# A two-layer diffusion backbone: q of the next HGRN2 head projected ahead of its gates, and a 32-byte tile at the right end of SBUF

## The chip, the cores and the metric

The kernel runs on one core of a Trainium2 chip. Its time is the device time of one execution in microseconds (us), and the figure for the kernel before is the median of three runs. The profile is of one further execution, whose own time stands beside it below.

A core has five engines with an instruction queue each: TensorE (PE in the profile; PEld is its weight load), VectorE (DVE), ScalarE (ACT), GpSimd (POOL) and SyncE (SP, which here issues DMAs). SBUF is the on-chip memory of 128 partitions, and an address below is a byte offset in each partition. PSUM is the memory into which TensorE accumulates.

## The reference

Two layers work on 1024 latent tokens and 256 context tokens of width 1024. Layer 0 runs neighbourhood attention heads and mLSTM heads side by side. Layer 1, which the change touches, has 16 HGRN2 heads with key and value widths of 128, and only its latent tokens are an output:

```python
q, f_fwd, f_bwd, i, z = split(h @ w_in)              # 5 x 2048 columns; 128 of each per head
f = lb + (1 - lb) * sigmoid(f_pre)                   # per direction
k, lf = 1 - f, log(f)
q = silu(q)
# each direction d: the state over the context tokens, then chunk by chunk over the latent tokens
o = q exp(b) @ S + (causal pairs q exp(b_t - b_s) k) @ v;   S = exp(b_L) S + (k exp(b_L - b))^T v
out = rms(o_fwd + o_bwd) * h_norm * silu(z)
x = x + gate * (concat(out) @ w_out)
```

Here b is the running sum of lf. The kernel works with products of f instead of sums of its logarithm.

## The kernel before

**Projections.** Matmuls of large operands are done in three products: an operand is split into a high part and a low part, and `dense` (L125 to L131) issues high x high (L128), high x low (L129) and low x high (L130) for each of 8 blocks of 128 rows. The modulated input of a layer stands in `hh` and `hl` (8 x 1280 columns). `proj_tr` (L143) keeps a 128-column slab of the weight stationary and moves `hh`/`hl`, 256 or 512 tokens at a time; the profile names these matmuls mm<-hh,wh (the moving operand comes first). `proj_nat` (L134) keeps tokens stationary and moves the weight (mm<-wh,hh, mm<-wzh,hh).

**Weights.** `wring` loads a weight of 128 columns in two pieces of four row blocks. A piece is a DMA on SP's queue into a raw buffer (three of them), a cast on ACT into a tile `wh` (L72) and a subtraction on DVE into `wl` (L73). In layer 1 these tiles are a ring of four of each on the right side of SBUF (pool w1); in layer 0 the ring is on the left side (pool w0). The v and z columns of a head have tiles of their own on the left side (`wz`).

**SBUF.** Pools are laid from the left or from the right end. `hh` and `hl` are on the right side, and so are the ring of layer 1 and the pool `oy` of the output projections (tiles wo, y, oacc). Before, hh starts at 147424 in one layer and 131040 in the other; the ring's first tiles of layer 1 are at 221152 and 227296. All of these are 32 more than a multiple of 64. The tiles on the left start at multiples of 64.

**A head.** The loop (L1339 to L1352) does for each head:

- `hg_intra`: K = 1 - F from the gates F of both directions (L972), Q = q x F (L979), 16 small "strips" s<-gq,gkn (L997) for the pairs nearest to each other, and then seven levels (`hg_level`), each with an ACT copy of K (gksel, L1024), 16 strips s<-gQ,gksel, a copy under a mask (L1042), and the updates of K and Q by the products of f (L1050, and T at L1052).
- `hg_vz`: the projection of v and z: 24 matmuls mm<-hh,wz for the context's v (its transposes tr<-ident,gEc come later), then 8 tiles of tokens with 24 mm<-wz,hh each. `hg_close` transposes K (L1009).
- `hg_ctx`: the state over the context. Its k lies in a buffer of the tag gq, which has two buffers, shared with the two halves of q. The transposes are L954, the copy gknc L956, the matmuls s<-gv,gknc L961.
- `hg_scan`: the states chunk by chunk (L1062 and L1078 on PE, L1064 and L1080 on DVE) and the outputs (acc, L1073 to L1075). For each half of the chunks four squares on ACT (L1089) give sums gss, POOL takes them to the power -1/2 (L154, L156), and DVE multiplies the output by it and by z (gz, L1093).
- `hg_proj` for the next head: six projections of gates (per direction 256 context tokens and twice 512 latent tokens, 24 matmuls each, a sigmoid L899 and a scaling L900), then q (twice 512 latent tokens, a sigmoid L908 and a multiply L909).
- `hg_out`: transposes of gz (L1133), an ACT copy gyt (L1135) and a store.
- `wo_sums` (L1101 to L1116): work for the end of the kernel on POOL's queue, loads of quarters of the output weight into the buffers gknc and gEc, subtractions and stores; one per head for heads 0 to 7, two for heads 8 to 11. `y_diff` (heads 1 to 8) is similar.

Afterwards `hh` and `hl` are freed, and the output projection (L835 to L837) runs with loads into `oy`.

**Order.** A tile scheduler orders the instructions of every engine: it goes by the order of the program text as priority and by a timeline of its own of when operands and buffers come free. So the matmuls of a head's projections stand between the strips and transposes of the head before it. PSUM has two banks for projections (mm), two for transposes (tr), three for s and one for acc. The gates have one buffer each (gF, gFc), and so have gK, gQ, gEc and gknc.

Of the kernel before, what the change touches and what calls it, by code (L numbers as in the profile page):

```python
# [9 lines left out]
F32 = mybir.dt.float32  # L10
F32R = mybir.dt.float32r
U8 = mybir.dt.uint8
AF = mybir.ActivationFunctionType
ALU = mybir.AluOpType
# [4 lines left out]
P = 128  # L19
D = 1024  # L20
KD = D // P
LAT = 1024
CTX = 256
# [21 lines left out]
class Prog:  # L45
# [836 lines left out]
    def hg_proj(self, h, pool, w=None):  # L882
        nc, a = self.nc, self.a
        st = {}
        col = lambda i: a["wc"][:, i * 2048 + h * P : i * 2048 + (h + 1) * P]
        lb, olb = self.lb[:, 0, h : h + 1], self.lb[:, 1, h : h + 1]
        F = self.t(self.fp, [P, 2, LAT], F32, "gF", 1)
        Fc = self.t(self.fp, [P, 2, CTX], F32, "gFc", 1)
        todo = [(d, t0, n) for d in range(2) for t0, n in ((LAT, CTX), (512, 512), (0, 512))]
        if w:  # L890

            todo.sort(key=lambda x: x[1] == 0)
        w = w or [None, None]
        for d, t0, n in todo:
            w[d] = w[d] or self.wring([col(1 + d)], P)
            ps = self.ps("mm", [P, n])
            self.proj_tr(ps, w[d], 0, t0, n)
            dst = Fc[:, d, :] if t0 == LAT else F[:, d, t0 : t0 + 512]
            nc.scalar.activation(dst, ps, AF.Sigmoid)  # L899
            nc.vector.tensor_scalar(out=dst, in0=dst, scalar1=olb, scalar2=lb, op0=ALU.mult, op1=ALU.add)  # L900
        q = {}
        w = self.wring([col(0)], P)
        for t0 in (512, 0):
            ps = self.ps("mm", [P, 512])
            self.proj_tr(ps, w, 0, t0, 512)
            q[t0 // 512] = self.t(pool, [P, 512], F32, "gq", 2)
            sg = self.t(pool, [P, 512], F32, "gsg", 1)
            nc.scalar.activation(sg, ps, AF.Sigmoid)  # L908
            nc.vector.tensor_tensor(out=q[t0 // 512], in0=sg, in1=ps, op=ALU.mult)  # L909
        return dict(F=F, Fc=Fc, q=q)  # L910

    def hg_vz(self, h, st, pool):
# [55 lines left out]
    def hg_intra(self, st, pool):  # L968
        nc = self.nc
        F, q = st["F"], st["q"]  # L970
        K = self.t(pool, [P, 2, LAT], F32, "gK", 1)
        nc.vector.tensor_scalar(out=K, in0=F, scalar1=-1.0, scalar2=1.0, op0=ALU.mult, op1=ALU.add)  # L972
        Q = self.t(pool, [P, 2, LAT], F32, "gQ", 1)
        ks = [self.t(pool, [P, 512], F32, "gkn", 4) for _ in range(2)]
        for hf in (1, 0):
            s = slice(hf * 512, (hf + 1) * 512)
            nc.vector.tensor_tensor(out=ks[hf], in0=K[:, 0, s], in1=K[:, 1, s], op=ALU.add)
            for d in range(2):
                nc.vector.tensor_tensor(out=Q[:, 1 - d, s], in0=q[hf], in1=F[:, d, s], op=ALU.mult)  # L979
        hv = dict(Q=Q, K=K, T=F, D=self.t(pool, [P, 8, 64], F32, "gD", 1))  # L980
        hv["A"] = self.t(pool, [P, 8, P], F32, "gA", 1)
# [157 lines left out]
    def build(self):  # L1139
        tc, nc, a = self.tc, self.nc, self.a  # L1140
        dma = nc.sync.dma_start
        with ExitStack() as es:
# [22 lines left out]
            def load(name, shape, eng=nc.gpsimd):  # L1165
# [12 lines left out]
                out=self.qkn, in0=qkn[:, 0:1], scalar1=qkn[:, 1:2], scalar2=0.125, op0=ALU.mult, op1=ALU.mult  # L1178
# [3 lines left out]
            sg = self.t(cp, [P, KD, 2], F32, "sct")  # L1182
# [10 lines left out]
            for i in range(2):  # L1193
# [6 lines left out]
                out=self.lb[:, 1, :], in0=self.lb[:, 0, :], scalar1=-1.0, scalar2=1.0, op0=ALU.mult, op1=ALU.add  # L1200
            )


            right = ExitStack()
            es.enter_context(right)
            self.open_h(right)
# [76 lines left out]
            with tc.tile_pool(name="op0", bufs=2) as op, ExitStack() as wl:  # L1283
# [27 lines left out]
                right = es.enter_context(ExitStack())  # L1311
# [22 lines left out]
            with l1:  # L1334
                pool = l1.enter_context(tc.tile_pool(name="hg", bufs=2))
# [32 lines left out]
                w = block(W[0:D, 0:512], wo * 8, None, [self.rawp, 3, "wraw"])  # L1368
                self.out_part(w, 0, 0, y2, yp, lambda t, ps: nc.scalar.copy(acc[0][:, t, :], ps))
                w = block(self.sw[1], wr * 4 + wo * 4)  # L1370
# [233 lines left out]
```

## Time and profile before

| | us |
|---|---|
| median of three runs | 3487.19 (3485.26 to 3489.89) |
| the profiled execution, its own time | 3489.74 |
| its span in the profile | 3488.0 |
| busy: PE / DVE / ACT / POOL | 3409.5 / 2098.0 / 1478.0 / 707.3 |
| first strips of head 0 | at 1898.3 |
| first strips of head 15 | at 3248.1 |

The mean granted clock of TensorE in that execution was 0.993 of full speed. A row of a timeline reads: start, duration, engine, line, operation, out<-in, tile shape and count, and in brackets the idle time before it with what ended it. A row of a group reads: line, engine, operation, operands, shape, count, then busy time, mean ns, and the idle time before them. An instruction's duration of a matmul reaches over its successor's start, so that the time which a matmul costs is read from the distance between starts.

### The profile page before, as it was taken

How to read it: one execution, taken by the hardware profiler on the slowest of the kernel's cores; microseconds unless marked ns; L12 is line 12 of the kernel's file. 1: busy time of each engine (PE TensorE's matmuls, PEld its weight loads, DVE VectorE, ACT ScalarE, POOL GpSimd, SP SyncE). 2: the span in 40 equal slices, each digit the busy share in tenths (PEclk: the TensorE clock that was granted, in tenths of full speed). 3: DMA queues.
4: the chain of work that ended last, by engine and by line, in shares of the span. 5: the costliest groups of instructions: out<-in, count | busy, mean ns of one | idle time of the engine just before them, and what ended most of it. 6: DMA issues, size and time to landing. Idle time of an engine off the chain costs nothing.

```text
span 3488.0 us, 64893 instructions
## 1 busy us (share of the span) xinstructions
PE 3409.5 (98%) x25100; PEld 2990.6 (86%) x25100; DVE 2098.0 (60%) x4855; ACT 1478.0 (42%) x3433; POOL 707.3 (20%) x1076
## 2 busy tenths in 40 slices
PE   8999999999999999999999999999999999999997
PEld 5679998889989888898888988988888888888876
DVE  4546665666655566777666555555555555555667
ACT  5445554554543444454354333333333333333442
POOL 2222221222111112221100112222223222100023
PEclk9999999999999999999999999999999999999999
DMA  5542222322233434444752111111112111110274
GB/s 202 175 130 61 79 77 76 91 78 75 79 89 99 145 117 127 132 129 143 218 162 70 46 58 55 58 59 58 57 57 67 61 58 49 49 37 31 85 233 151
DMA packets 331540, 333.60 MB, mean 96 GB/s; under 512 B 30984, under 2 KB 277960, under 8 KB 331232
## 3 DMA queue, kind: packets, MB, share of 16 engines
q1 hardware_dynamic: 291008, 222.76, 22.0%
q0 software_dynamic: 40224, 106.69, 9.0%
q8 instruction: 198, 3.24, 0.4%
q14 instruction: 110, 0.90, 0.1%
HBM read 259.40 MB, written 69.79 MB: 94 GB/s over the span
## 4 chain that ended last, share of the span: by engine, by line
PE 85%; DMA 4%; issue 3%; DVE 3%; POOL 2%; ACT 1%; SPq 0%; POOLq 0%; DVEq 0%; ACTq 0%
PE mm L128 18%; PE mm L129 18%; PE mm L130 18%; PE s L997 4%; PE acc L775 2%; PE mm L837 2%; PE mm L835 2%; PE mm L836 2%; PE tr L755 2%; PE acc L547 2%; PE s L556 2%; PE acc L537 1%; PE tr L1009 1%; PE acc L1073 1%; PE acc L1074 1%
## 5 line engine op out<-in xcount | busy, mean ns | idle before, releaser
L128 PE MATMUL mm<-hh,wh 128*128 128x512 f32 (+1 forms) x1600 | 584.5, 365 | 0.0
L129 PE MATMUL mm<-hl,wh 128*128 128x512 f32 (+1 forms) x1600 | 584.3, 365 | 0.0
L130 PE MATMUL mm<-hh,wl 128*128 128x512 f32 (+1 forms) x1600 | 583.5, 365 | 0.0
L128 PE MATMUL mm<-wh,hh 128*128 128x256 f32 (+1 forms) x1520 | 471.2, 310 | 1.7 <-ACT ev L317 0.6
L129 PE MATMUL mm<-wl,hh 128*128 128x256 f32 (+1 forms) x1520 | 469.9, 309 | 0.0
L130 PE MATMUL mm<-wh,hl 128*128 128x256 f32 (+1 forms) x1520 | 468.9, 309 | 0.3 <-DVE hl L262 0.3
L130 PEld LDWEIGHTS mm<-hh,wl 128*128 128x128 f32 x1600 | 301.3, 188 | 45.6 <-issue 0.6
L129 PEld LDWEIGHTS mm<-hl,wh 128*128 128x128 f32 x1600 | 301.6, 188 | 43.8 <-issue 0.2
L128 PEld LDWEIGHTS mm<-hh,wh 128*128 128x128 f32 x1600 | 301.6, 188 | 43.0 <-issue 0.2
L128 PEld LDWEIGHTS mm<-wh,hh 128*128 128x128 f32 x1520 | 286.5, 189 | 16.5 <-issue 0.9
L129 PEld LDWEIGHTS mm<-wl,hh 128*128 128x128 f32 x1520 | 286.5, 188 | 14.7 <-issue 2.9
L130 PEld LDWEIGHTS mm<-wh,hl 128*128 128x128 f32 x1520 | 286.4, 188 | 13.8 <-issue 1.5
L128 PE MATMUL mm<-wzh,hh 128*128 128x256 f32 x1024 | 292.8, 286 | 0.6 <-ACT gz L934 0.6
L129 PE MATMUL mm<-wzl,hh 128*128 128x256 f32 x1024 | 292.8, 286 | 0.0
L130 PE MATMUL mm<-wzh,hl 128*128 128x256 f32 x1024 | 291.5, 285 | 0.0
L73 DVE TENSOR_TENSOR wl<-wraw,wh 128x512 fp32r<-128x512 f32 x240 | 165.5, 694 | 129.2 <-ACT wh L72 121.5
L72 ACT CAST wh<-wraw 128x512 fp32r<-128x512 f32 x240 | 147.2, 618 | 198.9 <-PE mm L129 140.7
L1024 ACT COPY gksel<-gK 128x1024 f32<-128x1024 f32 x112 | 128.0, 1143 | 213.0 <-PE s L997 139.2
L128 PEld LDWEIGHTS mm<-wzh,hh 128*128 128x128 f32 x1024 | 193.5, 189 | 3.8 <-ACT gz L934 1.6
L129 PEld LDWEIGHTS mm<-wzl,hh 128*128 128x128 f32 x1024 | 193.4, 189 | 1.0
L130 PEld LDWEIGHTS mm<-wzh,hl 128*128 128x128 f32 x1024 | 193.3, 189 | 1.0
L835 PE MATMUL mm<-woh,yh 128*128 128x512 f32 x422 | 170.4, 404 | 9.8 <-DVE og L1366 5.2
(390 smaller groups left out, 7623.4 us busy)
## 6 DMA issues: line engine op xcount, KB each, us to landing
wraw<-in_wab_dram SPq DMA_DIRECT2D x112, 256.0 KB
wraw<-in_wc_dram SPq DMA_DIRECT2D x96, 256.0 KB
wraw<-yd SPq DMA_DIRECT2D x94, 256.0 KB
adar<-in_wada_dram POOLq DMA_DIRECT2D x32, 512.0 KB, 4.5
wraw<-in_wc_dram SPq DMA_DIRECT2D x128, 128.0 KB
md<-ev POOLq DMA_DIRECT2D x60, 256.0 KB, 2.8
mloz<-md SPq DMA_DIRECT2D x40, 256.0 KB
adar<-in_wada_dram SPq DMA_DIRECT2D x16, 512.0 KB
```

The costliest lines, as they stand in the source:

```text
L72: nc.scalar.copy(hi, x)
L73: nc.vector.tensor_tensor(out=lo, in0=x, in1=hi.bitcast(F32), op=ALU.subtract)
L128: mm(ps, lhsT=lh(k), rhs=rh(k), start=(start and k == 0), stop=False)
L129: mm(ps, lhsT=lh(k), rhs=rl(k), start=False, stop=False)
L130: m = mm(ps, lhsT=ll(k), rhs=rh(k), start=False, stop=(stop and k == nk - 1))
L547: nc.tensor.matmul(num, lhsT=qc[:, j, :], rhs=C[d][:, j, :], start=False, stop=(j == 1))
L556: nc.tensor.matmul(u, lhsT=st["k"][c][:, j * P : (j + 1) * P], rhs=vw, start=True, stop=True)
L755: nc.tensor.transpose(pt[:nk, i, :], pr[:, o : o + nk], self.ident)
L775: m = nc.tensor.matmul(yp[h64], lhsT=v[:, h64], rhs=pTs[hd][:nk, i, :], start=(i == turn[0]), stop=(i == turn[-1]), tile_position=(0, hd * ...
L835: mm(ps, lhsT=yh[k], rhs=w.h(kk), start=(kk == 0), stop=False)
L997: self.nc.tensor.matmul(out[s], lhsT=lhsT, rhs=rhs, start=True, stop=True, tile_position=(0, b * 64))
L1024: nc.scalar.copy(ksel.rearrange("p (b s i) -> p b s i", s=2, i=h), pick(K))
```

## The change

It has two parts.

In `hg_proj` the q projection becomes an inner function `swish()`. Its instructions are the same: a weight slab of 128 columns with its two loads, casts and subtractions, 48 matmuls of 512 columns, two sigmoids and two multiplies. For heads 1 to 15 (no weight handed in) it is called ahead of the six gate projections; for head 0, whose gate weights are loaded earlier and handed in, it stays behind them.

In `build` a pool `edge` is opened on the right side ahead of `hh` and `hl`, with one tile of 8 fp32 columns (32 bytes in each partition), which DVE sets to zero once. All that lies on the right side moves down by 32 bytes: hh to 147392 and 131008, the ring's first tiles in layer 1 to 221120 and 227264. The tiles on the left stay where they were.

The number of instructions on each engine is the same but for that one on DVE.

```diff
--- before.py
+++ after.py
@@ -884,12 +884,27 @@
         st = {}
         col = lambda i: a["wc"][:, i * 2048 + h * P : i * 2048 + (h + 1) * P]
         lb, olb = self.lb[:, 0, h : h + 1], self.lb[:, 1, h : h + 1]
+        q = {}
+
+        def swish():
+            w = self.wring([col(0)], P)
+            for t0 in (512, 0):
+                ps = self.ps("mm", [P, 512])
+                self.proj_tr(ps, w, 0, t0, 512)
+                q[t0 // 512] = self.t(pool, [P, 512], F32, "gq", 2)
+                sg = self.t(pool, [P, 512], F32, "gsg", 1)
+                nc.scalar.activation(sg, ps, AF.Sigmoid)
+                nc.vector.tensor_tensor(out=q[t0 // 512], in0=sg, in1=ps, op=ALU.mult)
+
+        todo = [(d, t0, n) for d in range(2) for t0, n in ((LAT, CTX), (512, 512), (0, 512))]
+        if w:
+
+            todo.sort(key=lambda x: x[1] == 0)
+        else:
+            swish()
         F = self.t(self.fp, [P, 2, LAT], F32, "gF", 1)
         Fc = self.t(self.fp, [P, 2, CTX], F32, "gFc", 1)
-        todo = [(d, t0, n) for d in range(2) for t0, n in ((LAT, CTX), (512, 512), (0, 512))]
-        if w:
-
-            todo.sort(key=lambda x: x[1] == 0)
+        first = w
         w = w or [None, None]
         for d, t0, n in todo:
             w[d] = w[d] or self.wring([col(1 + d)], P)
@@ -898,15 +913,8 @@
             dst = Fc[:, d, :] if t0 == LAT else F[:, d, t0 : t0 + 512]
             nc.scalar.activation(dst, ps, AF.Sigmoid)
             nc.vector.tensor_scalar(out=dst, in0=dst, scalar1=olb, scalar2=lb, op0=ALU.mult, op1=ALU.add)
-        q = {}
-        w = self.wring([col(0)], P)
-        for t0 in (512, 0):
-            ps = self.ps("mm", [P, 512])
-            self.proj_tr(ps, w, 0, t0, 512)
-            q[t0 // 512] = self.t(pool, [P, 512], F32, "gq", 2)
-            sg = self.t(pool, [P, 512], F32, "gsg", 1)
-            nc.scalar.activation(sg, ps, AF.Sigmoid)
-            nc.vector.tensor_tensor(out=q[t0 // 512], in0=sg, in1=ps, op=ALU.mult)
+        if first:
+            swish()
         return dict(F=F, Fc=Fc, q=q)
 
     def hg_vz(self, h, st, pool):
@@ -1201,6 +1209,8 @@
             )
 
 
+            edge = es.enter_context(tc.tile_pool(name="edge", bufs=1, side="right"))
+            nc.vector.memset(self.t(edge, [P, 8], F32, "edge"), 0.0)
             right = ExitStack()
             es.enter_context(right)
             self.open_h(right)
```

More of the change, by code (lines that the diff above doesn't have):

```diff
@@ L886, in hg_proj @@
         lb, olb = self.lb[:, 0, h : h + 1], self.lb[:, 1, h : h + 1]
-        F = self.t(self.fp, [P, 2, LAT], F32, "gF", 1)
-        Fc = self.t(self.fp, [P, 2, CTX], F32, "gFc", 1)
+        q = {}
[8 more added lines that the diff above has]
+                nc.vector.tensor_tensor(out=q[t0 // 512], in0=sg, in1=ps, op=ALU.mult)
         todo = [(d, t0, n) for d in range(2) for t0, n in ((LAT, CTX), (512, 512), (0, 512))]
@@ L892, in hg_proj @@
             todo.sort(key=lambda x: x[1] == 0)
+        else:
+            swish()
+        F = self.t(self.fp, [P, 2, LAT], F32, "gF", 1)
+        Fc = self.t(self.fp, [P, 2, CTX], F32, "gFc", 1)
+        first = w
         w = w or [None, None]
```

## The prediction

> **What bounds the kernel now.** I read the page first: the busy shares, then the chain of waits.
>
> ```profile
> PE 3409.5 (98%) x25100; PEld 2990.6 (86%) x25100; DVE 2098.0 (60%) x4855; ACT 1478.0 (42%) x3433; POOL 707.3 (20%) x1076
> PE 85%; DMA 4%; issue 3%; DVE 3%; POOL 2%; ACT 1%; SPq 0%; POOLq 0%; DVEq 0%; ACTq 0%
> ```
>
> TensorE is busy for 98% of the span and holds 85% of the chain that ended last. Both programs issue the same matmuls, so the change can act in three ways: on the time from one matmul to the next, on the few places where PE waits, and on the clock. Next comes the view by stretches, cut where a head's first strips start (columns: length; busy time of PE, PEld, DVE, ACT, POOL; clock; DMA share; GB/s).
>
> ```profile
> 1898.30:2698.80 800.50, 789.64 (x7016) 717.38 (x7016) 450.88 (x734) 281.61 (x583) 172.76 (x235) 1.00 0.18 57
> 2254.10:2343.10 89.00, 87.44 (x781) 79.44 (x780) 50.54 (x83) 31.70 (x66) 19.94 (x27) 1.00 0.18 57
> 2698.80:3160.10 461.30, 451.06 (x3893) 404.91 (x3892) 254.34 (x415) 158.20 (x331) 85.29 (x126) 0.99 0.16 50
> 3160.10:3248.10 88.00, 86.45 (x773) 78.46 (x772) 47.45 (x79) 29.44 (x62) 8.37 (x11) 1.00 0.08 25
> 3248.10:3488.00 239.90, 212.76 (x1229) 173.26 (x1228) 167.76 (x241) 92.98 (x180) 63.07 (x59) 0.95 0.55 170
> 2794.10:2797.40 3.30, 3.30 (x18) 3.30 (x17) 0.87 (x3) 0.86 (x2) 0.00 (x0) 0.50 0.00 0
> ```
>
> Row one is heads 0 to 8, row two one of them (head 4), row three heads 9 to 13, row four head 14, row five head 15 and the last projection. A steady head takes 89.0 us, but heads 9 to 13 take 461.3 / 5 = 92.3. The last row is a piece of head 10 in which the granted clock was 0.50.
>
> In a steady head PE waits once. The timelines of PE, ACT, POOL and DVE:
>
> ```profile
> 2261.52 0.39 PE L1075 MATMUL acc<-gS,gQ 128*128 128x128 f32 x2
> 2266.47 0.49 PE L1133 MATMUL tr<-ident,gz 128*128 128x128 f32 x3
> 2268.40 1.18 PE L997 MATMUL s<-gQ,gksel 128*64 128x64 f32 x32 [1.45 <-DVE gQ L1050]
> ```
> ```profile
> 2262.01 0.28 ACT L1089 ACTIVATE gjk<-acc 128x128 f32<-128x128 f32 x1 [1.79 <-PE acc L1075]
> ```
> ```profile
> 2263.98 1.36 POOL L156 TENSOR_TENSOR gss<-gss,mhalf 128x4 f32<-128x4 f32 x1
> ```
> ```profile
> 2265.38 1.13 DVE L1093 SCALAR_TENSOR_TENSOR gz<-acc,gss,gz 128x128 f32<-128x128 f32 x4 [0.59 <-POOL gss L156]
> 2267.03 1.22 DVE L1050 TENSOR_TENSOR gQ<-gQ,gF 128x1024 f32<-128x1024 f32 x1
> ```
>
> The previous head's last accumulation (2261.52) starts a chain: squares on ACT, the power on POOL, four gz multiplies on DVE, and behind these gQ's update for level 1. Only six transposes stand on PE between the strips of level 0 and those of level 1, so PE waits 1.45 us.
>
> Heads 9 to 13 have a second wait, from POOL's queue (PE, then POOL):
>
> ```profile
> 2792.73 0.81 PE L1133 MATMUL tr<-ident,gz 128*128 128x128 f32 x3 [1.87 <-DVE gz L1093]
> ```
> ```profile
> 2771.00 1.13 POOL L1109 DMA_DIRECT2D gknc<-in_woc_dram  x2 [40.52 <-ACT gsg L908]
> 2789.61 0.19 POOL L154 TENSOR_SCALAR gss<-gss 128x4 f32<-128x4 f32 x1 [1.85 <-ACT gjk L1089]
> 2789.88 0.73 POOL L1110 TENSOR_TENSOR gEc<-gEc 128x256 f32<-128x256 f32 x1
> 2791.17 1.03 POOL L156 TENSOR_TENSOR gss<-gss,mhalf 128x4 f32<-128x4 f32 x1
> 2792.17 0.59 POOL L1116 DMA_DIRECT2D sw<-gEc  x1
> ```
>
> From head 8 to 11 two wo_sums are issued per head. Here they hold POOL from 2771.0 to 2792.8, 21.8 us, and a subtraction and a store stand between the two halves of gss. PE waits 1.87 us, and the 0.50 clock follows at 2794.1: 3.4 us at half speed lose 1.7.
>
> **The change, part by part.** *Order.* I compared the two built programs: TensorE's instructions are the same up to head 1's first gate, and SP's for its first 918 of 1014. In a steady head, runs of matmuls of one kind go from 58 to 65. I priced every pair of neighbours by its mean start-to-start time over heads 2 to 8 of the trace, some 780 matmuls each; no single row shows these prices, but their sum can be held against one: before's order costs 87.49 us a head by them, with the wait of 1.45 it is 88.94, and row two has 89.0. After's order costs 88.90: seven more switches at 0.2 us each, 1.41. In after, 35 wz matmuls stand between the two levels, 35 x 0.117 = 4.1 us (spacing below) in place of six transposes, and that covers the 1.45. So **a steady head gains next to nothing**: the wait is turned into switches. Heads 0 to 8 come to 801.3 against 800.5: +0.8.
>
> For heads 9 to 13, after's order is priced at 447.7 against 461.3, **-13.6**, if POOL's wait and the half clock behind it go. What speaks for it: wo_sums starts when the gknc matmuls have freed its buffer, and in after these stand before four of the six gates instead of before one gate and the q. From there to the first half's last accumulation I price 25 us instead of 19.5, against 21.8 of wo_sums; POOL's order puts all of it ahead of gss. Head 14 is priced at 89.6 against 88.0, +1.6. The end (row five) gets 203.3 against 201.0 by the same prices, and hh comes free some 1 us later for the last projection's buffers: +3.3, with 6 either way, since the DMA share of that stretch is 0.55 and its waits are not priced.
>
> *What is late next.* The gates come last now, and the level-0 strips need K from both:
>
> ```profile
> L977 DVE TENSOR_TENSOR gkn<-gK 128x512 f32<-128x512 f32 x2 | 1.7, 850 | 0.0
> L1052 DVE TENSOR_TENSOR gT<-gF 128x1024 f32<-128x1024 f32 x1 | 1.2, 1222 | 0.0
> L972 DVE TENSOR_SCALAR gK<-gF 128x2048 f32<-128x2048 f32 x1 | 1.2, 1219 | 0.0
> L944 DVE MEMSET gEc<- 128x1 f32 x1 | 0.1, 59 | 0.0
> ```
>
> Sigmoid and bound (about 1.2) and K, T0 and two gkn (1.22 + 1.22 + 2 x 0.85) make some 6 us; 45 matmuls of 0.117 and some 20 short ones, about 7.8 us, cover them. Without cover each microsecond costs 15 over the heads. The gz transposes move into the strips of level 0: from the last accumulation 11 strips, 35 wz and 8 strips, some 5.6 us, stand ahead of them, against 2266.47 - 2261.52 = 4.95 in the rows, a margin of 0.7. The second q half waits for the transposes of gq, since they share a buffer, and gknc's copy has only four matmuls of cover; both are within 0.3 us of fitting. I take **+2** for such waits, with ends 0 and +15 (1 us a head). The q slab's loads move ahead of the gates' loads; the rows below show no idle time before hh,wh, so they are not what is late. The memset is 59 ns by its nearest row, once, at the start.
>
> *The 32 bytes.* By the allocated addresses hh, hl and all right-hand weights lie at 32 modulo 64 and go to 0; the left-hand ones (layer 0's ring, wz) lie at 0 and stay. So pairs that agreed still agree, and pairs that differed come to agree. First and last starts of unbroken runs: 512 columns that differ (layer 0), 512 that agree (head 4), 256 that differ (layer 0), 256 that agree (head 4), wz, which differs, and w moving, which differs (layer 0):
>
> ```profile
> 263.16 0.39 PE L128 MATMUL mm<-hh,wh 128*128 128x512 f32 x1
> ...
> 267.59 0.39 PE L129 MATMUL mm<-hl,wh 128*128 128x512 f32 x1
> ```
> ```profile
> 2288.22 0.39 PE L128 MATMUL mm<-hh,wh 128*128 128x512 f32 x1
> ...
> 2292.98 0.39 PE L128 MATMUL mm<-hh,wh 128*128 128x512 f32 x1
> ```
> ```profile
> 272.34 0.28 PE L128 MATMUL mm<-hh,wh 128*128 128x256 f32 x1
> ...
> 274.67 0.28 PE L130 MATMUL mm<-hh,wl 128*128 128x256 f32 x1
> ```
> ```profile
> 2283.38 0.28 PE L128 MATMUL mm<-hh,wh 128*128 128x256 f32 x1
> ...
> 2285.88 0.28 PE L128 MATMUL mm<-hh,wh 128*128 128x256 f32 x1
> ```
> ```profile
> 1999.74 0.28 PE L129 MATMUL mm<-wzl,hh 128*128 128x256 f32 x1
> ...
> 2002.31 0.28 PE L130 MATMUL mm<-wzh,hl 128*128 128x256 f32 x1
> ```
> ```profile
> 1499.98 0.28 PE L128 MATMUL mm<-wh,hh 128*128 128x256 f32 x1
> ...
> 1500.81 0.28 PE L129 MATMUL mm<-wl,hh 128*128 128x256 f32 x1
> ```
>
> 4.43/19 = 233 ns against 4.76/21 = 227: at 512 columns agreeing is some 6 ns shorter. 2.33/20 = 116.5 and 2.57/22 = 116.8 against 2.50/21 = 119.0: at 256 it is some 2.4 **longer**. With w moving the short run gives 0.83/7 = 118.6, so less is to be lost there; over longer stretches I take 118.2. Counts by form, one of three lines each:
>
> ```profile
> L128 PE MATMUL mm<-hh,wh 128*128 128x512 f32 x1152 | 458.1, 398 | 0.0
> L128 PE MATMUL mm<-wh,hh 128*128 128x256 f32 x1280 | 371.8, 291 | 1.2 <-ACT ev L317 0.6 <-ACT ev L634 0.3 <-ACT hh L261 0.2
> L128 PE MATMUL mm<-wzh,hh 128*128 128x256 f32 x1024 | 292.8, 286 | 0.6 <-ACT gz L934 0.6
> ```
>
> Of 512 columns that come to agree there are 1152 in layer 0 (the other 2304 are HGRN2's, which agree already), 960 with w or wx moving and some 550 in the output projections: about 2660 x 5.2 (the mean over longer stretches is nearer 5) = -13.7. Of 256: 3072 of wz x 2.3, 3840 of w moving x 0.8 and 960 others (hh or hl moving by 256) x 1.8: +11.9. Net **-1.8**, with ends -14 (256 columns don't mind) and +7 (only they do).
>
> [...]
>
> **Sum:** 0.8 - 13.6 + 1.6 + 3.3 + 2 - 1.8 = -7.7. The profiled execution took 3489.74 (span 3488.0) and comes to 3482.0; the median of the runs is 2.55 lower, so 3487.2 - 7.7 = **3479.5**.
>
> **The rivals.** *The POOL wait stays* (wo_sums still reaches into gss). Before loses 12.2 over its own prices in heads 9 to 13; that kept makes 3479.5 + 12.2 = 3491.7. For it: POOL's wo_sums is unchanged, and the margin is 25 - 21.8.
>
> *Slower:* the gz transposes, now amid the level-0 strips, come due before DVE has gz, as at 2792.73. A wait of 1.9 followed by a half-clock stretch costs 1.9 + 1.7 = 3.6 a head: over 15 heads 54 us, 3533; in half of them 3506. It decides from the point at which the chain is 0.7 us longer than the rows have it, and the total passes +7 at the fifth head. Against it: the 1.45 waits of the steady heads are followed by a clock of 1.00. [...]
>
> *Alignment counts at 512 only:* -14 instead of -1.8, 3467.3.
>
> [...]
>
> **How the numbers follow.** Forecast as summed 0.36, POOL wait kept 0.19, slower 0.20, 512 only 0.15, no alignment 0.10. Some 0.2% (7 us) is what a measurement of this kernel can tell from no change: under 3480.2 is faster, over 3494.2 slower. The forecast and the no-alignment case lie at the bound; I count 0.30 of their 0.46 as faster, with the 0.15 of 512 only and 0.04 of the POOL case, in which other terms help: 0.49. Slower: 0.20 and 0.06 of the POOL case: 0.26. Same: 0.25. The range goes from the 512-only case less 3 of the tail's 6 (3464) to the slower case with four to five heads (3501); the steep part of that case is left out. The likeliest case's own range is 3472 to 3487.
>
> **What would show it.** Heads 9 to 13 at 89 to 90 us without 0.50 stretches; no wait before level 1 in steady heads, which stay at 89; layer 0's 512-column spacing at 227 and wz's at 119. It is wrong if a new wait on DVE gz or gQ appears in every head, if switches cost more than their pairs did, or if wz keeps 117.

## The result, and the profile after

The changed kernel took 3496.83 us (median of 8 runs, 3493.53 to 3499.87). The kernel before, run on the same occasions, took 3486.04 (8 runs, 3481.57 to 3489.89). The ratio is 1.0031, with a 95% interval of 1.0020 to 1.0042: **slower by 0.3%**, where the prediction had 7.7 us faster. The profiled execution of the changed kernel took 3496.75 us, close to its median. That of before (3489.74) lay 3.7 above its own median, so the two profiles differ by 7.0 us of span and the medians by 10.8.

The page of the changed kernel, the two rows shown first of before:

```profile
PE 3428.6 (98%) x25100; PEld 3001.0 (86%) x25100; DVE 2093.7 (60%) x4856; ACT 1473.4 (42%) x3433; POOL 709.7 (20%) x1076
PE 86%; DMA 5%; issue 3%; DVE 3%; ACT 1%; SPq 0%; POOL 0%; POOLq 0%; DVEq 0%; ACTq 0%
```

TensorE has the same 25100 matmuls and 19.1 us more busy time, and POOL is gone from the chain of waits (2% before). The view by stretches, cut as before (heads 0 to 8; head 4; heads 9 to 13; head 14; head 15 and the end), and a short stretch of head 12:

```profile
1893.20:2697.10 803.90, 803.72 (x7023) 720.69 (x7023) 447.55 (x736) 278.73 (x585) 171.41 (x239) 1.00 0.18 57
2250.30:2339.50 89.20, 89.20 (x780) 79.80 (x778) 50.08 (x84) 31.18 (x66) 18.74 (x26) 1.00 0.18 57
2697.10:3154.40 457.30, 449.65 (x3876) 400.81 (x3874) 250.42 (x415) 155.93 (x329) 90.14 (x122) 1.00 0.16 49
3154.40:3245.80 91.40, 89.80 (x778) 79.92 (x776) 48.41 (x80) 28.84 (x62) 9.29 (x10) 1.00 0.08 24
3245.80:3495.00 249.20, 216.74 (x1233) 175.98 (x1232) 170.06 (x242) 93.61 (x180) 61.83 (x58) 0.93 0.53 164
3018.90:3022.30 3.40, 2.97 (x35) 2.69 (x36) 2.70 (x4) 1.79 (x4) 0.00 (x0) 0.52 0.18 55
```

Beside the rows of before this is the difference between the two profiled executions, and it is complete:

| stretch | before | after | difference | forecast of the order's terms |
|---|---|---|---|---|
| up to head 0 | 1898.3 | 1893.2 | -5.1 | (none; addresses -1.8 in all) |
| heads 0 to 8 | 800.5 | 803.9 | +3.4 | +0.8 |
| heads 9 to 13 | 461.3 | 457.3 | -4.0 | -13.6 |
| head 14 | 88.0 | 91.4 | +3.4 | +1.6 |
| head 15 and the end | 239.9 | 249.2 | +9.3 | +3.3 |

Two of these rows hold more than the change. The start of head 0 differs between kernels that are the same up to there: before has it at 1898.3, and four of the kernels below with its addresses (`e2_order`, `e5_raw4`, `e6_low`, `e8_not15`) between 1893.6 and 1896.2, with 3 to 6 us less idle time of PE ahead of it. And in heads 9 to 13 before's execution has four stretches of 3.4 us at half the clock and after's one; at 1.7 us lost in each, that is 5.1 us of difference by itself.

Read the steady head first. In after PE is busy for 89.20 of 89.20 us; before it was busy for 87.44 of 89.00. **The wait is gone, PE is never idle, and the head takes longer.** PE's busy time rose by 1.76 us for the same matmuls: a matmul's duration in these rows seems to include what it loses behind another kind of matmul, so that waits turned into switches look like work (an estimate; the section on the prediction has the sums). The timeline of PE in that head shows where the wait went:

```profile
2250.90 0.49 PE L1083 MATMUL acc<-gS,gQ 128*128 128x128 f32 x2
2256.48 0.89 PE L1005 MATMUL s<-gQ,gksel 128*64 128x64 f32 x16
2257.29 0.33 PE L1141 MATMUL tr<-ident,gz 128*128 128x128 f32 x1
2258.97 0.33 PE L1141 MATMUL tr<-ident,gz 128*128 128x128 f32 x1
2264.21 1.21 PE L1005 MATMUL s<-gQ,gksel 128*64 128x64 f32 x32
```

From the last accumulation to the first gz transpose there are now 6.4 us, and the strips of level 1 (2264.21) have no bracket of idle time behind them. Over heads 0 to 14 the view of waits of PE in after is short (columns: total, times, longest):

```profile
PE s L1005 <- DVE gQ L1058: 9.2, 6, 2.7
PE s L1005 <- DVE gq L897: 1.0, 1, 1.0
```

There is no wait for gz any more, in heads 9 to 13 either, and POOL holds up nothing. But six waits for gQ are there, one in each of heads 9 to 14, and at a place that the prediction did not look at. Head 12, where the longest is; ACT, DVE, PE and SP:

```profile
3016.10 0.62 ACT L72 CAST wzh<-wraw 128x512 fp32r<-128x512 f32 x1 [2.65 <-DMA wraw<-in_wc_dram]
```
```profile
3016.76 0.69 DVE L73 TENSOR_TENSOR wzl<-wraw,wzh 128x512 fp32r<-128x512 f32 x1 [3.08 <-ACT wzh L72]
3017.37 0.72 DVE L1050 COPY_PREDICATED gD<-glm,s 128x512 f32<-128x512 uint8 x1
3017.98 1.21 DVE L1058 TENSOR_TENSOR gQ<-gQ,gT 128x1024 f32<-128x1024 f32 x1
```
```profile
3019.33 0.91 PE L1005 MATMUL s<-gQ,gksel 128*64 128x64 f32 x12 [2.68 <-DVE gQ L1058]
```
```profile
3011.76 6.08 SPq L101 DMA_DIRECT2D wraw<-in_wc_dram  x5
```

The bracket on PE names DVE's update of gQ, but DVE itself sat idle for 3.08 us before that, with a subtraction of a **weight piece** (wzl) at the head of its queue; ACT's cast of the piece (wzh) waited 2.65 us for its load. gQ's update had nothing to do with the weight. It only stood behind it in DVE's queue. And the 2.68 us of idle PE were followed by 3.4 us at a clock of 0.52, row six above.

### The profile page after: what moved, and what is told of

It is laid out like the page before. It is cut to its first block, busy times and chain, and to the rows that moved or that the text cites. A ratio compares the mean times of both kernels' runs of the same rounds, so it can differ in the third digit from the quotient of the medians.

```text
span 3495.0 us, 64916 instructions
## 1 busy us (share of the span) xinstructions
PE 3428.6 (98%) x25100; PEld 3001.0 (86%) x25100; DVE 2093.7 (60%) x4856; ACT 1473.4 (42%) x3433; POOL 709.7 (20%) x1076
## 4 chain that ended last, share of the span: by engine, by line
PE 86%; DMA 5%; issue 3%; DVE 3%; ACT 1%; SPq 0%; POOL 0%; POOLq 0%; DVEq 0%; ACTq 0%
PE mm L128 18%; PE mm L129 18%; PE mm L130 18%; PE s L1005 5%; PE acc L775 2%; PE mm L835 2%; PE mm L837 2%; PE mm L836 2%; PE tr L755 2%; PE acc L547 2%; PE s L556 2%; DMA wraw<-in_wc_dram 1%; PE acc L537 1%; PE tr L1017 1%; PE acc L1083 1%
```

## The experiments

All are compared with the kernel before on the same chip. Differences are of medians. `e1` to `e4` ran on one chip, `e5` to `e9` on a second and `f1` to `f4` on a third; before's medians there are 3485.96, 3485.06 and 3485.26, so a difference between kernels of two chips carries about 1 us more of doubt. A trace is of one execution, which can lie some us off the median of its kernel.

### The two parts alone

`e1_edge` has the tile and the order of before; `e2_order` has the order and no tile:

```diff
+            edge = es.enter_context(tc.tile_pool(name="edge", bufs=1, side="right"))
+            nc.vector.memset(self.t(edge, [P, 8], F32, "edge"), 0.0)
```

> Only the 32-byte tile, with the order of before. Theory A (addresses help, order costs): head 0 starts 5.1 us earlier, as in the changed kernel, wz at 256 columns falls from 117.0 to 115.8 ns (3072 of them, -3.7), the rest of layer 1 keeps its pace: about 9 us shorter than before, a ratio near 0.9974. Theory B (the loss in the last projection comes with the shifted tiles): only the 5.1 and 3.7 are gained and the end is 9 us longer: no change, ratio near 1.000. In theory B the first strips of head 15 to the last matmul take some 238 us, in theory A some 229.

> Only q ahead of the gates, without the tile: all addresses as before. Theory A: head 0 starts where it did before (1898), steady heads take 89.2 to 89.5 instead of 88.95, heads 9 to 14 show the waits of 1 to 3 us of the strips for gQ, the end is 9 us longer: 15 to 20 us longer than before, a ratio near 1.005. Theory B: the order gives back some 2 us, 3484, a ratio near 0.9995.

The tile alone: 3479.04 us against 3485.96, ratio 0.9982 (0.9974 to 0.9991), **6.9 us faster**. The order alone: 3502.31, ratio 1.0054 (1.0040 to 1.0068), **16.3 us slower**. The two make +9.4, and the changed kernel +10.8. So theory A holds in sign and roughly in size, and theory B falls: with the tile alone the end takes its usual time (229.5 us from head 15's first strips to the last matmul, 228.7 before). Two signs of theory A did not come: head 0 starts at 1896.7 with the tile alone, only 1.6 earlier than before instead of 5.1, and at 1894.6 with the order alone, where before's 1898 was expected. So the -5.1 of the table above is not the work of the addresses alone. The stretches of the order alone (heads 0 to 8, 9 to 13, 14, the end):

```profile
1894.60:2700.80 806.20, 806.07 (x7023) 722.96 (x7023) 446.83 (x736) 279.15 (x585) 170.52 (x239) 1.00 0.18 57
2700.80:3160.20 459.40, 451.43 (x3876) 402.23 (x3874) 250.55 (x415) 155.99 (x329) 90.21 (x122) 1.00 0.16 49
3160.20:3251.90 91.70, 90.20 (x778) 80.33 (x776) 48.48 (x80) 28.85 (x62) 9.24 (x10) 1.00 0.08 24
3251.90:3498.10 246.20, 216.82 (x1233) 175.89 (x1231) 167.78 (x242) 93.93 (x180) 63.57 (x58) 0.94 0.53 166
```

Against before +5.7, -1.9, +3.7 and +6.3: every stretch but heads 9 to 13 loses.

### The late weight piece

`e5_raw4`: the order alone, with a fourth raw buffer for weight pieces in layer 1 (the tail's first block, which uses the same buffers, has it too):

```diff
-            rw = rawp if isinstance(rawp, list) else (rawp or self.rawp, rawb, rawt)
+            rw = rawp if isinstance(rawp, list) else (rawp or self.rawp, self.nraw or rawb, rawt)
...
                 self.rawp = pool
+                self.nraw = 4
```

> The order change alone (addresses as before) with four raw buffers for weight pieces in layer 1 instead of three. Theory C: the strips' waits for gQ in heads 9 to 14 (1.1 to 3.0 us, 10.9 in sum) come from a wz piece that lands late, because its load starts only when a raw buffer is free; ACT's cast and DVE's subtraction stand ahead of gQ's update. With a fourth buffer the loads start earlier and the waits go: 3502 - 11 = 3491. Rival D: the pieces are late for another reason (SP's queue, the time a load takes): the waits stay, 3502 within 3.

It took 3486.54 (before 3485.06), ratio 1.0007 (0.9998 to 1.0015): 15.8 us faster than the order alone, somewhat more than the 11 expected. In heads 9 to 13 PE has no idle time left (busy 449.50 of 449.50, against 451.43 of 459.40):

```profile
2700.70:3150.20 449.50, 449.50 (x3877) 401.01 (x3875) 251.22 (x415) 155.45 (x329) 90.42 (x122) 1.00 0.16 50
```

So it was the number of raw buffers that set when the load could start, and theory C holds. Heads 0 to 8 keep their 805.6 us, and so does the end most of its length (233.4 us to the last matmul; 235.0 in the order alone, 228.7 before): these have another cause.

### Which heads lose

`e6_low` projects q first for heads 1 to 8 only, `e8_not15` for heads 1 to 14 (there with `h < 15`); both are without the tile:

```diff
-        else:
+        late = w or not (h < 9)
+        if not late:
             swish()
...
-        if first:
+        if late:
             swish()
```

> The order change for heads 1 to 8 only; heads 9 to 15 project their gates first, as before. Theory C: the steady heads keep their 89.5 instead of 88.95 (switches), +5 in sum, and heads 9 to 14 and the end are as before: 3491, a ratio near 1.0015. Rival D (a head's length depends on what the heads before it did): heads 9 to 14 lose as in the order change alone, 3497 or more.

> The order change for heads 1 to 14; head 15 projects its gates first, as before. If the end (from head 15's first strips to the last matmul, 235 to 238 us instead of 229) is longer because of head 15's own order, it comes back to 229 and the time to 3495. Rival: what differs at the end is where DVE and POOL happen to collide in the last projection; then it stays between 229 and 238 without a rule, and the time at 3502.

`e6_low` took 3486.64, ratio 1.0004 (0.9995 to 1.0013), not the 3491 expected. Its steady heads are at 89.5 as foreseen (803.2 in all for heads 0 to 8, +2.7), but heads 9 to 13 took 457.4, 3.9 less than before. Its waits there are not the reason: three for gz make 6.6 us, before's four 6.3. The clock is: its execution has one stretch of 3.4 us at half the clock in these heads and before's four, which is 5.1 us. With that set apart theory C holds for heads 9 to 14, and rival D, 3497 or more, falls. `e8_not15` took 3491.16, ratio 1.0014 (1.0005 to 1.0023), **11.2 us less than the order alone by undoing one head**. Of that, 8 us are in the end of the two traces. Its end, and then the waits of PE in the end of the order alone and of this one:

```profile
3250.50:3488.80 238.30, 212.62 (x1230) 174.12 (x1228) 167.42 (x241) 93.32 (x180) 64.65 (x59) 0.95 0.56 172
```
```profile
PE mm L835 <- DVE og L1374: 7.8, 3, 4.0
PE mm L835 <- ACT yh L72: 5.3, 4, 1.8
PE mm L128 <- ACT yh L72: 1.6, 2, 1.1
```
```profile
PE mm L835 <- DVE og L1374: 4.1, 3, 2.3
PE mm L835 <- ACT yh L72: 0.8, 2, 0.4
```

The end is 238.3 instead of 246.2. What the last head lacks is work to hide behind. With its gates last, its levels finish 48.8 us after its first strips (43.2 before) and its last accumulation 102.8 after them (93.4 before; 92.8 in `e8_not15`); each later step, the store of y, its load and the cast to yh, is that much later, and the output projection runs into it: yh is waited for 6.9 us instead of 0.8.

### POOL's two wo_sums

`e9_spread` is the kernel before with one line changed:

```diff
-                    for i in ([h] if h < 8 else [2 * h - 8, 2 * h - 7] if h < 12 else []):
+                    for i in ([0, 1] if h == 0 else [h + 1] if h < 15 else []):
```

> The kernel before, with wo_sums spread: two in head 0, one in each of heads 1 to 14, instead of one in heads 0 to 7 and two in heads 8 to 11. If the second wo_sums of a head causes the waits of 1.9 us of the gz transposes in heads 9 to 13 and the half-clock stretches behind them, they go: 12 us, 3474, ratio 0.9965. Rival: they come from where the scheduler has put the heads' work, not from POOL: 3486 within 3.

It took 3475.5 against 3485.06, ratio 0.9972 (0.9960 to 0.9983), **9.6 us faster**. Heads 9 to 13 in the view by stretches:

```profile
2696.90:3141.60 444.70, 436.99 (x3894) 397.14 (x3896) 253.28 (x415) 158.47 (x330) 82.00 (x111) 1.00 0.16 48
```

That is 88.9 a head, as in the steady ones, 16.6 less than before (the prediction priced their loss at 12.2). No wait for gz and no half-clock stretch is left in them; before's four stretches are 6.8 of the 16.6. The end is 2 us longer. So the prediction's reading of the 461.3 was right, and the change was not needed to get at it.

### The place of operands

A tile of 96 bytes (24 columns), and a control of 64 bytes (16 columns):

```diff
-            nc.vector.memset(self.t(edge, [P, 8], F32, "edge"), 0.0)
+            nc.vector.memset(self.t(edge, [P, 24], F32, "edge"), 0.0)
```

> A tile of 96 bytes with the order of before: right-hand tiles at 0 modulo 64 as with 32 bytes, but hh at 0 modulo 128 instead of 64. If only the place modulo 64 counts, it takes what the 32-byte tile alone takes, within 0.1%. If 256-column matmuls are slow when both operands agree modulo 128 (120 ns in the head's context gates, 119.5 in layer 0 with 64 and 64) and fast when they differ by 64 (wz 115.8), then wz at 0 with hh at 0 goes to 119.5 (3072 x 3.7 = +11) and layer 0's w at 64 with hh at 0 falls from 119.5 to 115.8 (3840 x 3.7 = -14, and 576 x 3.5 = -2): about 5 us shorter than the 32-byte tile alone.

> A tile of 64 bytes with the order of before: right-hand tiles stay at 32 modulo 64. If the gain of layer 0 comes from the place modulo 64, nothing changes: ratio 1.000 within 0.1%, 512-column matmuls of layer 0 at 233 ns, wz at 117. If it came from the mere shift or from the added tile, it would gain the same 5 us ahead of head 0 as with 32 bytes.

96 bytes: 3478.75, ratio 0.9982 (0.9973 to 0.9990), the same time as 32 bytes. 64 bytes: 3486.17, ratio 1.0007 (0.9998 to 1.0016), no change. By the times alone both expectations of "modulo 64" stand. What did not come is the 5 us that 96 bytes should have gained by the other theory: w fell to 117.1 ns, not to 115.8. **The traces of the control speak against modulo 64.** Its head 0 starts at 1890.3, 8 us earlier than before: 4.4 of it at w moving by 256 columns, and 3.4 because before's execution has half-clock stretches at 1596 and 1746 and the control's none there. In the heads wz is slower, 119.7 ns against 117.0, and heads 0 to 8 take 804.4 us against 800.5. Then a test of wz alone, `f4_wzpad`: the 32-byte tile, and a pad of 64 bytes ahead of wz, which moves wz (and what is allocated behind it) from 0 to 64 modulo 128.

```diff
+        if h == 0:
+            nc.vector.memset(self.t(pool, [P, 16], F32, "pad", 1), 0.0)
         w = self.wblock(pool, "wz", [col(3), col(4)], KD, 256)
```

> The 32-byte tile with order of before, and a pad of 64 bytes ahead of wz, so that wz lies at 64 modulo 128, as hh does. If the place modulo 128 decides, wz goes from 116.3 to 119.5 ns (3072 x 3.2 = +10): 3489. If modulo 64 decides, nothing changes: 3479.

3486.95, ratio 1.0006 (0.9997 to 1.0014): 7.9 us more than the tile alone (which ran on another chip), by a shift that modulo 64 cannot see. The two profiled executions lie at the far ends of their kernels' runs, so that their spans do not show it; heads 0 to 8 do, 803.3 us against 799.6. First and last starts of unbroken runs of wz, two of the changed kernel (wz at 0, hh at 64), then one of this kernel (both at 64):

```profile
1984.79 0.28 PE L129 MATMUL mm<-wzl,hh 128*128 128x256 f32 x1
...
1988.67 0.28 PE L129 MATMUL mm<-wzl,hh 128*128 128x256 f32 x1
```
```profile
1992.67 0.28 PE L128 MATMUL mm<-wzh,hh 128*128 128x256 f32 x1
...
1996.41 0.28 PE L128 MATMUL mm<-wzh,hh 128*128 128x256 f32 x1
```
```profile
1992.18 0.28 PE L130 MATMUL mm<-wzh,hl 128*128 128x256 f32 x1
...
1996.09 0.28 PE L130 MATMUL mm<-wzh,hl 128*128 128x256 f32 x1
```

3.88/33 = 117.6 and 3.74/33 = 113.3 ns against 3.91/33 = 118.5. With wz at 0 and hh at 64 whole runs go at 113.3 or at 117.8 (in the tile alone 17 and 30 of its 47 runs of 24 matmuls or more); with both at 64 none is under 118. What picks one of the two paces is not known, so the means below, 116.3 among them, are of a mixture. Over all neighbouring starts of one form (gaps with other work in them left out), with the places of the moving and the stationary operand modulo 128:

| moving / stationary | 512 columns, ns | 256 columns, ns |
|---|---|---|
| equal (96/96, 64/64, 0/0, 32/32; hh moving) | 228.3 to 228.7 | 119.4 to 119.5 |
| hh moving: 96/64 (before), 0/64 (96 bytes), 32/64 (64 bytes) | 233.2, 233.1, 232.9 | 117.2, 115.6, 118.3 |
| w moving: 64/96, 64/64, 64/0, 64/32 (before, 32, 96, 64 bytes) | 232.9, 229.7, 229.9, 233.0 | 118.4, 119.5, 117.1, 117.0 |
| wz moving: 0/96, 0/64, 0/0, 0/32 (before, 32, 96, 64 bytes), 64/64 (`f4_wzpad`) | | 117.0, 116.3, 118.6, 119.7, 118.8 |

At 512 columns equal places are some 5 ns shorter with hh moving and 3 with w moving; but w at 64 with hh at 0 (229.9) is as short as equal places. At 256 columns equal places are mostly the slow ones, and 64 apart is fast; 0/32 (119.7) fits no rule that I have.

### The gains put together

`f1_spread_edge` joins the tile and the spread wo_sums in before's order. `f2_mod128` has wo_sums spread, the tile of 96 bytes and the pad ahead of wz. `f3_mended` is the changed kernel with four raw buffers, head 15 as before, and wo_sums spread. All their edits are shown above.

> The kernel before with the 32-byte tile and with wo_sums spread over heads 0 to 14: both gains stand in different places, so they add: 3475.5 - 6.9 = 3469, a ratio near 0.995. If the tile's gain depended on the waits of heads 9 to 13, it would stay at 3475.

> wo_sums spread, a tile of 96 bytes at the right end (hh at 0 modulo 128) and a pad of 64 bytes ahead of wz (wz at 64 modulo 128), order of before. If the place modulo 128 decides: wz moving at 64 with hh at 0 takes 117.1 (as layer 0's w did in the 96-byte run) instead of 118.6, the context gates of layer 1 stay at 119.4, layer 0's w at 117.1 instead of the 119.5 of the 32-byte tile: some 5 us below the 96-byte tile with spreading (3475.5 - 7.2 - 4.6 = 3464). If only modulo 64 counts, it equals the spread kernel with the 32-byte tile.

> The changed kernel with its three faults mended: four raw buffers, head 15 with gates first, wo_sums spread. If the order change is a loss of its own (seven more switches a head that cost more than the wait of 1.45 they replace), steady heads stay at 89.2 instead of 88.85 and it is 5 us or more slower than the spread kernel with the tile: 3474 or more. If the loss was only in the faults, it equals it, 3469, or beats it.

| kernel | us | ratio to before (95%) |
|---|---|---|
| `f1_spread_edge` | 3471.8 | 0.9963 (0.9951 to 0.9976) |
| `f2_mod128` | 3464.05 | 0.9940 (0.9926 to 0.9953) |
| `f3_mended` | 3475.44 | 0.9974 (0.9964 to 0.9983) |

`f2_mod128` came out at the 3464 that was worked out from the spacings, and beats both kernels: 21 us below before. `f1_spread_edge` is 2.8 us above the 3469 expected, within its interval, so that the hit of the other to the microsecond is in part luck. `f3_mended` is 3.6 us slower than `f1_spread_edge`, which has the same wo_sums and the same places modulo 128; that is less than the 5 expected, and the two intervals overlap. The heads tell them apart: heads 0 to 8 take 802.7 us and 799.6. One steady head of each, `f3_mended` first:

```profile
2251.50:2340.70 89.20, 89.20 (x781) 79.79 (x780) 50.07 (x84) 31.19 (x66) 18.95 (x26) 1.00 0.19 57
```
```profile
2246.10:2334.90 88.80, 87.27 (x782) 79.26 (x782) 50.58 (x83) 31.73 (x66) 19.62 (x27) 1.00 0.19 57
```

0.4 us a head with nothing waited for: what the order adds to PE's work is more than the wait that it removes.

## Why the prediction was wrong, point by point

**What bounds the kernel: right.** The waits that were read (1.45 us at level 1, 1.87 us behind POOL) went with the change, as forecast, and the spread wo_sums show that the second was worth 9.6 us by the medians and 16.6 in heads 9 to 13 of the two profiles, half-clock stretches included. The forecast took before's four half-clock stretches as fixed; in other traces that keep before's order in these heads there are from one (`e6_low`, `f4_wzpad`) to four (`e3_edge96`).

**The price of the order: too low.** The step that failed is "seven more switches at 0.2 us each, 1.41". At equal addresses (`f1_spread_edge` and `f3_mended`) PE's busy time rose from 87.27 to 89.20, 1.93 us or 0.28 for each of the seven. Start to start over heads 2 to 7 and with the idle time left out, neighbours of different kinds (by operands) take 12.63 us a head in the order alone and 10.55 before, neighbours of the same kind 76.87 and 76.84. Prices taken from before's order miss part of it: the mean distance between two 512-column matmuls of hh rose from 234.0 to 239.0 ns over 128 pairs a head, 0.64 us, and 1.41 + 0.64 is about the 2.1 measured. It stands in the pair *behind* the one that switches: the first takes 301 ns before and 308 in the order alone, later ones 229, and a head has 16 such firsts instead of 10. This is read from the trace; no run takes the switches apart. Heads 0 to 8 so came to +5.7 in the order alone, not +0.8.

**"What is late next": the failed step that weighed most.** The prediction bounded new waits at "+2, with ends 0 and +15", looked for them at level 0, and dismissed the weights: "the rows below show no idle time before hh,wh, so they are not what is late". That row tells only that PE never waits for a weight as its own operand. In after a weight piece's cast and subtraction stand ahead of gQ's update on ACT and DVE, and the strips wait for gQ. It cost 9.2 us in six heads (9.5 in the order alone), and the half-clock stretch behind head 12's costs 1.7 more; the fourth raw buffer took the waits away. So heads 9 to 13 came out 4.0 shorter instead of 13.6, and those 4.0 are less than the 5.1 that before's three further half-clock stretches cost. Why heads 1 to 8 have no such wait was not tried.

**The end: right sign, wrong size.** +3.3 with 6 either way was forecast, +9.3 came (+6.3 in the order alone). The working counted when hh comes free; what counted is when the last head's output is stored, 9 us later, with no next head to hide it. That is shown by undoing head 15 alone. In the profiled execution of after PE also waited 6.9 us in the stretch in which an addition of DVE took 5.88 us beside four of POOL (below).

**The 32 bytes: right sign, too small, one term with the wrong sign.** -1.8 was forecast, -6.9 came with the tile alone. The interval of the ratio makes that 3.1 to 9.1, and the traces locate only some 3 of it. From start to start, tile alone against before and ahead of head 0: hh and hl moving at 512 columns -4.8 (1152 x 5.2 = -6.0 in the forecast), w and wx moving at 512 -2.2 (960 x 5.2 = -5.0), w moving at 256 +4.9 (3840 x 0.8 = +3.1), hh and hl moving at 256 +1.2. In the heads wz was to lose 7.1 and gained some 2 (3072 x 0.7): classes modulo 64 were the wrong ones, since wz at 0 and hh at 64 "agree" modulo 64 and differ modulo 128. Where the rest of the 6.9 comes from stays open. That the tile does nothing had a chance of 0.10 (the forecast without its -1.8, 3481.3). It fell: the tile alone has a ratio of 0.9982 with an interval below 1, and layer 0's 512-column matmuls of hh went from 233.1 to 228.8 ns.

**The rivals.** The slower one named the gz transposes amid the level-0 strips. They had 6.4 us of cover and never waited: the right side, the wrong place. Its price of a wait with the half clock behind it (3.6) met one head, head 12 (2.68 and then 3.4 us at 0.52, 4.4). The POOL wait did not stay. The time, 3496.8, is in the range, but by luck: the range reached past no change for the slower rival, with a chance of 0.2, and what made the time is other than that rival's cause.

## What to carry to other kernels

When a change moves work ahead of other work, list for each in-order queue what now stands ahead of the instruction that PE needs, weight casts too: a wait is named after the last instruction (gQ's update in head 12, 2.68 us), and its cause may be a load two queues away (there ACT's cast waited 2.65 us for a weight piece, and DVE stood idle for 3.08 us behind the cast). Covering a wait of 1.45 us with more interleaving has its own price: here PE's busy time grew by 1.93 us a head with the same instructions. The last pass of a loop has no next one to hide behind and wants its own order: undoing one head of fifteen gave back 11 us here, 8 of them in the end. The parts do not add: the fourth buffer gave 15.8 and the last head 11.2 of a loss of 16.3.

## What the runs showed of the hardware that was not expected

- **Where operands start modulo 128 bytes changes the pace of matmuls** by 2 to 5 ns of 117 to 233, in opposite directions for 256 and 512 columns (table above). The rule is not complete: within one pair of places whole runs go at 113.3 or 117.8 ns. Two kernels that differ in a pad of 64 bytes differ by 7.9 us, and a control by total time alone can hide two such effects that cancel (in `e4_edge64` 4.4 us gained ahead of head 0 and 3.9 lost in heads 0 to 8, at a ratio of 1.0007).
- **Short waits and the clock.** In before, waits of 1.87 us in heads 10 to 12 were each followed by 3.4 us at half the clock; in after, one of 2.68 was, and the five others of heads 9 to 14 (9.2 - 2.7 = 6.5 us together) were not. Length alone does not decide. In `f4_wzpad` the first wait of 1.87 below was followed by a clock of 1.00 and the second, in the next head, by 0.50; in `e8_not15` even one of 2.96 was not followed by a half clock:

```profile
2880.44 0.30 PE L1135 MATMUL tr<-ident,gz 128*128 128x128 f32 x1 [1.87 <-DVE gz L1095]
2972.06 0.42 PE L1135 MATMUL tr<-ident,gz 128*128 128x128 f32 x1 [1.87 <-DVE gz L1095]
```
```profile
2880.50:2883.90 3.40, 3.38 (x27) 3.10 (x28) 1.44 (x6) 0.95 (x2) 0.00 (x0) 1.00 0.11 39
2972.10:2975.50 3.40, 3.40 (x16) 3.21 (x17) 0.94 (x4) 0.37 (x1) 0.00 (x0) 0.50 0.11 39
```
```profile
3025.95 0.28 PE L1005 MATMUL s<-gQ,gksel 128*64 128x64 f32 x2 [2.96 <-DVE gQ L1058]
```

The half-clock stretches of one execution lie on a grid: in before they start at 2794.04, 2886.20, 2978.36 and 3084.17, which is 27, 27 and 31 times 3.413 us apart, and one lasts one or more such steps. Of the waits of 1.87 to 1.91 us for gz in all traces, the eleven that fell inside one step (to 0.01 us) were followed by the half clock at its end. Of those cut by the grid, four left less than 1.5 us in either step (0.57 and 1.30, 1.38 and 0.49 in `f4_wzpad`; 0.99 and 0.88 in `e4_edge64`; 1.36 and 0.52 in `e6_low`) and had none, as had the 2.96 (1.42 and 1.54); one with 1.63 in a step (`e3_edge96`) had it. So the same wait can cost 1.7 us more in one execution than in another (3.4 us at half the clock). No exact bound comes out: in before's head 13 a wait of 1.74 for gQ (to 3079.70) lay inside a step and had no half clock behind that step, and one of 1.50 (to 3083.83) in the next step had.
- **DVE against POOL at the end.** In the changed kernel two additions of DVE took 6.48 us beside four of POOL, 5.88 of it the first; the others of this line took 0.68 to 1.83 (0.68 to 1.79 in before). PE waited 6.9 us for the next result. DVE and POOL:

```profile
3428.12 6.48 DVE L1427 TENSOR_TENSOR oys<-oyz,oys 128x512 f32<-128x512 f32 x2
3435.13 0.68 DVE L1427 TENSOR_TENSOR oys<-oyz,oys 128x512 f32<-128x512 f32 x1
```
```profile
3428.52 4.93 POOL L1376 TENSOR_TENSOR oacc<-os,oacc 128x512 f32<-128x512 f32 x4
```

DVE's first addition started at 3428.12, 0.40 us ahead of POOL's first, and ended at 3434.00, 0.55 us behind POOL's fourth (3433.45): in this stretch POOL's four took 1.25 to 1.28 us each, and DVE finished none. Why was not tried. One addition of 5.9 us stands in the ends of `e5_raw4`, `f1_spread_edge` and `f2_mod128` too. How much of the end is decided by such meetings was not tried.
